# A decoder trunk in float32: all gate and up pairs by seven products, their weight sums formed on chip by accumulating transfers

## The chip, the cores and the metric

The kernel runs on one core of a Trainium2 chip. The core has TensorE (matmul, PE in the profile), VectorE (DVE), ScalarE (ACT), GpSimd (POOL) and SyncE (SP); each of them works through its own instructions in order, and semaphores join them. SBUF and PSUM are the memories on chip, HBM the one outside. The metric is the time of one execution in microseconds (us) of device time, lower is better.

## The reference

Two layers over a residual stream of 512 positions by 1024 features, in float32: one with a short convolution, one with sliding-window attention. Behind each stands the same feed-forward block, and that is what the change is about. F is 2816.

```python
def swiglu(h, w_gate_up, w_down):
    g, u = jnp.split(h @ w_gate_up, 2, axis=-1)
    return (jax.nn.silu(g) * u) @ w_down
...
ff = swiglu(rmsnorm(h, ffn_pre_norm[l]), ffn_w_gate_up[l], ffn_w_down[l])
h = h + rmsnorm(ff, ffn_post_norm[l])
```

## The kernel before

**Arithmetic.** A float32 factor is split into a high and a low part that TensorE multiplies at its fast rate. ScalarE makes the high part (a copy with rounding), VectorE the low one (the difference). A product is then three matmuls: low by high, high by high, high by low (`mm3`, L190 to L192). So every weight tile that comes from HBM (a *raw* tile, 128 x 1024) needs one instruction of ScalarE (`whi`, L454) and one of VectorE (`wlo`, L455) before it can be used.

**Gate and up.** F is cut into 22 tiles of 128 features, two tiles to a pair, 11 pairs in a layer. A pair's weights can be seen as four blocks a, b, c, d, and its product with the activations x (also four blocks) can be made with seven block products in place of eight, in the manner of Strassen and Winograd. Each of the seven needs a block of x or a sum of its blocks (a *factor*), and a block of the weights or a sum of them. Factors 1, 2 and 3 are blocks of x. Factors 4 to 7 are sums: `keep` copies the blocks out of PSUM into `part` tiles (L351, L354) and `factors` makes the sums and splits them (L366 to L375). One product of a pair is a *job* of 24 matmuls of 256 columns. Products 1, 6, 7 and 4 add up in one accumulator (X), 5 and 3 in another (Z), 2 in a third (Y); between them `take` reads the accumulator's partial sums (L872 to L883), and the next product on it has to wait for that.

Before, `PLAIN = 4`: the first four feature tiles of a layer (two pairs) are plain products. `project_first` makes tiles 0 and 1 in halves of 256 columns, so that it can start while the last quarter of the positions is still being normed; `gate_plain` makes tiles 2 and 3 at 512 columns. The factors are made while tile 2 is multiplied. The other nine pairs are made by seven products (`gate_jobs`).

**Weight sums.** Four of a pair's seven weight factors are sums of blocks. `Sums` makes them in HBM by GpSimd's transfers, a copy and then accumulating transfers (L521), long before they are fetched; `BEGIN` says at which place in the program each pair's sums start. For six pairs in a layer (`ADDED`) only two of the four sums are made in HBM, and the others by an addition on VectorE onto a raw tile (L445).

**Order.** `in_line` works through the jobs in a list: with a job's products it issues the split of the job three places on (`LINE_LEAD = 3`), and fetches a raw tile as soon as one of the `N_RAW` buffers is free. The down products of a finished round of pairs stand behind the next pair. Around the layer's start the order is written out by hand (`manual_schedule`): `second_half` and `last_tile` finish the norm tile by tile (GpSimd's power operation, VectorE's update, ScalarE's scaled copy `xn`), `turn` transposes on TensorE into a PSUM bank, and `split` (L336, L337) reads that bank for the high and the low part of x.

Of the kernel before, what the change touches and what calls it, by code (L numbers as in the profile page):

```python
# [16 lines left out]
P = 128  # L17
# [7 lines left out]
PLAIN = 4  # L25

ADDED = (0, 1, 2, 6, 7, 8)

BEGIN = {
# [4 lines left out]
}  # L34

ADDED = (0, 1, 2, 6, 7, 8)

BEGIN = {
# [4 lines left out]
}  # L43
WARM = 8
LEAD = 2
LINE_LEAD = 3

EARLY_IN, REST_IN = 2, 0
# [8 lines left out]
N_SLOT, N_WIDE, N_RAW, N_W = 43, 14, 7, 4  # L57
# [17 lines left out]
def yoco_kernel(  # L75
# [10 lines left out]
    w_gu: bass.AP,  # L86
# [143 lines left out]
    class Update:  # L230
# [3 lines left out]
        def __init__(self, mix, gain, gpres, add):  # L234
            self.mix, self.gpres, self.add = mix, gpres, add
            self.gain = gain
# [93 lines left out]
        def split(self, n, f, hf):  # L330
            if self.x[n][f] is None:
                self.x[n][f] = (slot("xhi", F32R), slot("xlo", F32R))
            hi, lo = self.x[n][f]
            c = slice(hf * 256, (hf + 1) * 256)
            src = self.banks[f % 4, hf][:, (f // 4) * 256 : (f // 4 + 1) * 256]
            nc.scalar.activation(hi[:, c], src, AF.Copy, scale=g(self.gpres[n], f))  # L336
            nc.vector.scalar_tensor_tensor(  # L337
                out=lo[:, c], in0=src, scalar=g(self.gpres[n], f), in1=hi[:, c].bitcast(F32),
# [3 lines left out]
        def keep(self, b, hf, vector=False):  # L342

            for i in range(2):
                if (i, hf, b // 2) not in self.parts:
                    self.parts[i, hf, b // 2] = slot("part")
                out = self.parts[i, hf, b // 2][:, (b % 2) * 256 : (b % 2 + 1) * 256]
                src = self.banks[b, hf][:, i * 256 : (i + 1) * 256]
                gain = g(self.gpres[0], b + 4 * i)
                if vector:  # L350
                    nc.vector.tensor_scalar(out=out, in0=src, scalar1=gain, scalar2=None,  # L351
                                            op0=ALU.mult)
                else:
                    nc.scalar.activation(out, src, AF.Copy, scale=gain)  # L354

        def factors(self):


            x = self.x[0]
            made = {p: [] for p in range(1, 8)}  # L360
            for p, k0, c in ((1, 0, 0), (2, 4, 0), (3, 4, 256)):
                made[p] = [[a[:, c : c + 256] for a in x[k0 + k]] for k in range(4)]
            for j in range(2):
                q11, q21, q12, q22 = (self.parts[i, hf, j] for hf in range(2) for i in range(2))

                nc.vector.tensor_tensor(out=q11, in0=q11, in1=q12, op=ALU.subtract)  # L366
                nc.vector.tensor_tensor(out=q12, in0=q22, in1=q12, op=ALU.subtract)
                nc.vector.scalar_tensor_tensor(out=q22, in0=q22, scalar=-1.0, in1=q11,
                                               op0=ALU.mult, op1=ALU.subtract)
                nc.vector.scalar_tensor_tensor(out=q21, in0=q22, scalar=-1.0, in1=q21,  # L370
                                               op0=ALU.mult, op1=ALU.subtract)
                for p, q in ((6, q22), (5, q11), (7, q12), (4, q21)):
                    hi, lo = halves("xt", F32R)
                    nc.scalar.activation(hi, q, AF.Copy)
                    nc.vector.tensor_tensor(out=lo, in0=q, in1=hi.bitcast(F32),  # L375
                                            op=ALU.subtract)
                    made[p] += [[a[:, c : c + 256] for a in (hi, lo)] for c in (0, 256)]
# [36 lines left out]
    class Raw:  # L414


        def __init__(self, *srcs):
            self.srcs = srcs
            self.widths = [s.shape[0] * S if len(s.shape) == 3 else D for s in srcs]
            self.n = sum(self.widths)  # L420

# [9 lines left out]

    class Job:
# [6 lines left out]
        def __init__(self, raws, run, then=None, make=None):  # L439
            self.raws, self.run, self.then, self.make = raws, run, then, make  # L440

        def add(self):
            if self.make:
                raw = self.raws[0].tile
                nc.vector.tensor_tensor(out=raw, in0=raw, in1=self.raws[1].tile, op=ALU.add)  # L445

# [1080 lines left out]
```

## Time and profile before

| what | value |
|---|---|
| time, median of three runs | 1041.82 us |
| lowest of the three | 1040.96 us |
| span of the profiled execution | 1043.2 us, 17017 instructions |
| granted TensorE clock, mean | 0.997 |
| busy: TensorE, VectorE, ScalarE, GpSimd | 99%, 73%, 53%, 16% |
| moved by DMA | 221.48 MB, 212 GB/s in the mean |
| HBM read and written | 214.08 MB, 85.98 MB |

The profiled execution is one more execution than the three timed ones; its own time is known as its span, 1.4 us over their median, and durations of single instructions come from it. Columns of a row by line are: line of the kernel, engine, operation, what is written and read, shapes and count, then busy time and mean ns of one, then the idle time of that engine just before and what ended it. In the timeline a row is start, length, engine and instruction, with the idle time before it in brackets. A row with x8 joins eight instructions of one kind.

### The profile page before, as it was taken

The numbers are of one execution on the slowest core, as the hardware profiler recorded it, in microseconds if no ns is written. First come the engines' busy times: TensorE is split into PE (matmuls) and PEld (weight loads), VectorE is DVE, ScalarE is ACT, GpSimd is POOL, SyncE is SP. The second block draws the span as 40 slices with busy tenths as digits, with TensorE's granted clock in tenths as the row PEclk, the third lists the DMA queues.
The fourth block names the chain that finished last, engine by engine and source line by source line (L and its number), as shares of the span: only waits on it lengthen the run. The fifth ranks groups of instructions, "written<-read, shape, count | busy, mean of one in ns | idle before, by whom it ended". The sixth has DMA issues, their size and how long they took to land.

```text
span 1043.2 us, 17017 instructions
## 1 busy us (share of the span) xinstructions
PE 1031.6 (99%) x6556; PEld 931.4 (89%) x6556; DVE 761.4 (73%) x1280; ACT 552.5 (53%) x994; POOL 170.6 (16%) x227
## 2 busy tenths in 40 slices
PE   9999999999999999999999999999999999999997
PEld 7888888989879899999898888889998999989986
DVE  5675645488676978776658998685886777896754
ACT  7222235746645455464466777666565554645531
POOL 0322231122201000000021554211211110000001
PEclk9999999999999999999999999999999999999999
DMA  9657798568969955337413588967789697534521
GB/s 333 229 176 242 183 321 303 135 184 266 316 232 311 348 175 195 123 120 233 172 42 98 145 250 234 311 215 223 177 283 339 197 322 246 184 125 159 173 89 80
DMA packets 61297, 221.48 MB, mean 212 GB/s; under 512 B 7200, under 2 KB 8096, under 8 KB 51488
## 3 DMA queue, kind: packets, MB, share of 16 engines
q1 hardware_dynamic: 48608, 140.04, 37.2%
q0 software_dynamic: 12032, 79.70, 29.7%
q8 instruction: 51, 0.84, 0.3%
q10 hardware_dynamic: 576, 0.66, 0.2%
q14 instruction: 30, 0.25, 0.1%
HBM read 214.08 MB, written 85.98 MB: 288 GB/s over the span
## 4 chain that ended last, share of the span: by engine, by line
PE 89%; DVE 4%; DMA 3%; issue 1%; ACT 1%; POOLq 0%; POOL 0%; DVEq 0%; SPq 0%; ACTq 0%
PE gx L192 6%; PE gx L191 6%; PE gx L190 6%; PE pmix L191 5%; PE pmix L192 5%; PE pmix L190 5%; PE gz L192 3%; PE gz L191 3%; PE gz L190 3%; PE pgu L190 3%; PE pgu L191 3%; PE pgu L192 3%; PE px L190 2%; PE px L191 2%; PE px L192 2%; PE pcub L594 2%
## 5 line engine op out<-in xcount | busy, mean ns | idle before, releaser
L455 DVE TENSOR_TENSOR wlo<-raw,whi 128x1024 fp32r<-128x1024 f32 (+1 forms) x188 | 227.7, 1214 | 94.4 <-ACT whi L454 94.4
L454 ACT ACTIVATE whi<-raw 128x1024 fp32r<-128x1024 f32 (+1 forms) x188 | 194.6, 1049 | 82.7 <-DVE raw L445 26.6
L190 PE MATMUL gx<-xt,whi 128*128 128x256 f32 x432 | 122.3, 283 | 0.0
L191 PE MATMUL gx<-xt,whi 128*128 128x256 f32 x432 | 122.3, 283 | 0.0
L192 PE MATMUL gx<-xt,wlo 128*128 128x256 f32 x432 | 122.3, 283 | 0.0
L190 PEld LDWEIGHTS gx<-xt,whi 128*128 128x128 f32 x432 | 82.9, 192 | 0.0
L191 PEld LDWEIGHTS gx<-xt,whi 128*128 128x128 f32 x432 | 82.9, 192 | 0.0
L192 PEld LDWEIGHTS gx<-xt,wlo 128*128 128x128 f32 x432 | 82.9, 192 | 0.0
L521 POOL DMA_DIRECT2D hsum<-in_w_gb_dram x84 | 55.9, 717 | 120.5 <-ACT whi L454 81.0
L872 ACT ACTIVATE st<-gx 128x256 f32<-128x256 f32 x72 | 27.5, 381 | 84.2 <-PE gx L192 84.2
L289 POOL TENSOR_TENSOR ur<-uv,mhalf 128x1 f32<-128x1 f32 x15 | 11.6, 774 | 358.3 <-DVE uv L285 358.3
L185 ACT ACTIVATE whi<-raw 128x1024 fp32r<-128x1024 f32 x30 | 31.8, 1058 | 65.3 <-PE pb L191 26.3
L190 PE MATMUL pgu<-xlo,whi 128*128 128x256 f32 (+1 forms) x192 | 61.6, 321 | 0.0
L191 PE MATMUL pgu<-xhi,whi 128*128 128x256 f32 (+1 forms) x192 | 61.1, 318 | 0.0
L192 PE MATMUL pgu<-xhi,wlo 128*128 128x256 f32 (+1 forms) x192 | 61.1, 318 | 0.0
L186 DVE TENSOR_TENSOR wlo<-raw,whi 128x1024 fp32r<-128x1024 f32 x30 | 49.7, 1665 | 2.9 <-ACT whi L185 2.9
L190 PE MATMUL pmix<-wlo,ahi 128*128 128x512 f32 (+1 forms) x136 | 51.3, 377 | 0.0
L191 PE MATMUL pmix<-whi,ahi 128*128 128x512 f32 (+1 forms) x136 | 51.2, 377 | 0.0
L192 PE MATMUL pmix<-whi,alo 128*128 128x512 f32 (+1 forms) x136 | 51.2, 377 | 0.0
L521 POOL DMA_DIRECT2D hsum<-hsum x24 | 19.2, 825 | 153.2 <-ACT whi L454 87.8
L180 DVE TENSOR_TENSOR wlo<-raw,whi 128x512 fp32r<-128x512 f32 x50 | 33.8, 722 | 12.9 <-ACT whi L179 9.6
L190 PE MATMUL gz<-xlo,whi 128*128 128x256 f32 x144 | 40.8, 283 | 0.0
(279 smaller groups left out, 3201.5 us busy)
## 6 DMA issues: line engine op xcount, KB each, us to landing
hsum<-in_w_gb_dram POOLq DMA_DIRECT2D x84, 512.0 KB, 8.8
raw<-hsum SPq DMA_DIRECT2D x72, 512.0 KB, 8.0
raw<-in_w_gb_dram SPq DMA_DIRECT2D x54, 512.0 KB, 5.5
raw<-in_w_dn_dram SPq DMA_DIRECT2D x34, 512.0 KB, 4.8
hsum<-in_w_dn_dram POOLq DMA_DIRECT2D x24, 512.0 KB, 8.0
raw<-in_w_in_dram SPq DMA_DIRECT2D x21, 512.0 KB, 7.0
hsum<-hsum POOLq DMA_DIRECT2D x20, 512.0 KB, 7.4
hsum<-in_w_dn_dram POOLq DMA_DIRECT2D x12, 768.0 KB, 10.8
```

The lines of the kernel that those rows point to most:

```text
L180: nc.vector.tensor_tensor(out=lo[:, c], in0=raw[:, c], in1=hi[:, c].bitcast(F32), op=ALU.subtract)
L185: nc.scalar.activation(hi, raw, AF.Copy)
L186: nc.vector.tensor_tensor(out=lo, in0=raw, in1=hi.bitcast(F32), op=ALU.subtract)
L190: nc.tensor.matmul(out, whi, xlo, start=start, stop=False, **kw)
L191: nc.tensor.matmul(out, whi, xhi, start=False, stop=False, **kw)
L192: nc.tensor.matmul(out, wlo, xhi, start=False, stop=stop, **kw)
L289: nc.gpsimd.tensor_tensor(out=self.r[:, t : t + 1], in0=self.v[:, t : t + 1], in1=mhalf[:, :1], op=ALU.pow)
L454: self.begun = nc.scalar.activation(hi[:, :n], raw, AF.Copy)
L455: nc.vector.tensor_tensor(out=lo[:, :n], in0=raw, in1=hi[:, :n].bitcast(F32), op=ALU.subtract)
L521: nc.gpsimd.dma_start(dst, src, max_dma_last_dim=4 * 4 * S, **kw))
L594: nc.tensor.matmul(ps, (whi, whi, wlo)[i][:, kk], (xhi, xlo, xhi)[i], start=k == i == 0, stop=k == KT - 1 and i == 2)
L872: nc.scalar.activation(s, x, AF.Copy)
```

## The change

All 11 pairs go by seven products; the plain path and its weight array are gone. Pairs 0, 1, 2 and 3 are called A, B, C and D in the new tables, so that A5 is product 5 of pair 0. A class `Gates` holds a pair. The sums are formed on chip: a raw tile is fetched with block b, an accumulating transfer from GpSimd's queue adds block a to it (product 5), a second one c (product 6), a third d (product 3); another raw tile holds c (product 1) and then c + a (product 7). Each split reads the tile between two adds, and an add has to wait until both parts of the split before it have read the tile. For the *early* pairs A and B the sum of product 3 comes from HBM, the only gate sum still made there.

The splits go in an order of their own (`READY` for the opening, `SPLIT` for later pairs), the products in another (`OPENING`, then `PAIR`). `Line` holds up to five split weights ahead (`N_W`). The factors 5, 6, 7 and 4 are made one at a time between the products of the opening. The takes now cover both halves of a pair's accumulator at once.

```diff
-PLAIN = 4
-ADDED = (0, 1, 2, 6, 7, 8)
+PAIR = (1, 5, 6, 2, 7, 3, 4)
+SPLIT = {5: -2, 1: 0, 6: 2, 2: 3, 7: 4, 3: 6, 4: 8}
+OPENING = "A3 B3 C1 C2 A5 A6 B5 A7 B6 A4 C5 B7 C6 B4 C7 C3 C4"
...
-N_SLOT, N_WIDE, N_RAW, N_W = 43, 14, 7, 4
+N_SLOT, N_WIDE, N_RAW, N_W = 40, 14, 7, 5
...
+        def add_parts(self, j):
+            q11, q21, q12, q22 = (self.parts[i, hf, j] for hf in range(2) for i in range(2))
+            nc.vector.tensor_tensor(out=q11, in0=q11, in1=q12, op=ALU.subtract)
+            nc.vector.tensor_tensor(out=q12, in0=q22, in1=q12, op=ALU.subtract)
+            nc.vector.scalar_tensor_tensor(out=q22, in0=q22, scalar=-1.0, in1=q11,
+                                           op0=ALU.mult, op1=ALU.subtract)
+
+        def factor(self, p):
+            made = []
             for j in range(2):
...
+                if p == 4:
+                    nc.vector.scalar_tensor_tensor(out=q21, in0=q22, scalar=-1.0, in1=q21,
+                                                   op0=ALU.mult, op1=ALU.subtract)
+                q = {6: q22, 5: q11, 7: q12, 4: q21}[p]
+                hi, lo = halves("xt", F32R)
+                nc.scalar.activation(hi, q, AF.Copy)
+                nc.vector.tensor_tensor(out=lo, in0=q, in1=hi.bitcast(F32), op=ALU.subtract)
...
+        def add(self):
+            if self.jobs and self.jobs[0].more is not None:
+                tc.keep_in_program_order(
+                    nc.gpsimd.dma_start(self.tile, self.jobs[0].more, accum_op=ALU.add))
...
-                nc.vector.tensor_tensor(out=raw, in0=raw, in1=self.raws[1].tile, op=ALU.add)
...
+        def lo(self):
+            job = self.begun
+            job.lo()
+            self.held += not job.apart
+            job.raw.jobs.pop(0)
+            if job.raw.jobs:
+                job.raw.add()
+            else:
+                self.live -= 1
+            self.fetch()
+            return job
...
+        def fill(self):
+            while self.jobs and self.held < N_W:
+                job = self.one()
...
+        def run(self, jobs, late):
+            for job in jobs:
+                self.fill()
+                if job.run:
+                    job.run(job)
+                    self.held -= not job.apart
...
+                c, d, a, b = (w_gb[l, q, n] for n in range(4))
+                t1, t3 = Raw(b), Raw(c)
+                last = Raw(sums_of[f"h{l}{q}"].sums[0]) if early else t1
+                for p, raw, more in ((1, t3, None), (2, Raw(d), None), (5, t1, a), (6, t1, c),
+                                     (7, Raw(c) if early else t3, a),
+                                     (3, last, None if early else d), (4, Raw(b), None)):
+                    self.jobs[p] = Job(raw, self.run(p), None, more)
...
+                elif p == 6 and self.early:
+                    add(g1, x, g1)
+                    through(g1)
...
-                    for f in range(KT):
-                        before.split(0, f, 1)
-                    for b in range(4):
-                        before.keep(b, 1)
...
+                    for f in range(4):
+                        before.split(0, f + 4, 1)
+                        before.keep(f, 1, 0)
+                        before.keep(f, 1, 1, True)
+                    line.one()
+
+            for p, k0 in ((1, 0), (2, 4)):
+                for ks in ((0, 1), (2,), (3,)) if p == 1 else ((0,), (1,), (2,), (3,)):
+                    for gate in (a, b):
+                        gate.products(p, gate.jobs[p].w, ks)
...
+            early(a, ps_pt, lambda: None)
+            early(b, ps_sc, lambda: make(5))
+            gates[2].jobs[1].then = lambda: (make(6), a.take(2), b.take(2))[3:]
+            gates[2].jobs[2].then = lambda: make(7)
+            a.jobs[5].then = lambda: (make(4), sum_on(f"{l}f3"))[2:]
```

Three places in the order of the built programs follow, without times. The first is ScalarE in the kernel before, where the last quarter of the positions (`xt` banks 1682 to 1703) has been transposed, at layer 0's start:

```order
L336 ACTIVATE xhi_1568<-xt_1703,gt 128x256
L336 ACTIVATE xhi_1583<-xt_1682,gt 128x256
L336 ACTIVATE xhi_1591<-xt_1685,gt 128x256
L336 ACTIVATE xhi_1595<-xt_1700,gt 128x256
L336 ACTIVATE xhi_1601<-xt_1703,gt 128x256
L354 ACTIVATE part_1742<-xt_1682,gt 128x256
L354 ACTIVATE part_1744<-xt_1682,gt 128x256
L354 ACTIVATE part_1742<-xt_1685,gt 128x256
```

The same place on ScalarE after (`whi_1575` and `whi_1576` are halves of B3's weights, `whi_1634` is A5's, the banks are 1651 to 1672):

```order
L308 ACTIVATE xn_1573<-h_317,ur_1140 128x1024
L460 ACTIVATE whi_1575<-raw_1331 128x512
L460 ACTIVATE whi_1576<-raw_1331 128x512
L466 ACTIVATE whi_1634<-raw_1325 128x1024
L334 ACTIVATE x_1695<-xt_1651,gt 128x256
L351 ACTIVATE part_1698<-xt_1651,gt 128x256
L334 ACTIVATE x_1702<-xt_1654,gt 128x256
L351 ACTIVATE part_1698<-xt_1654,gt 128x256
L334 ACTIVATE x_1707<-xt_1669,gt 128x256
L351 ACTIVATE part_1710<-xt_1669,gt 128x256
```

Before, all splits of the last banks stand ahead of all copies to `part`; after, split and copy take turns on each bank, four splits in place of eight, and three halves or tiles of weights stand ahead of them.

The second place is VectorE after, where the factors of layer 0 are used up: takes of product 2 for A, B and C (`gr` from `gy`), factor 7 (`xt_1901`, `xt_1904`), the split of C5, the take of A5 (from `gz`), factor 4 and the split of B6, and at the end the take of A6 (`gr_1787` from `gx_1531`), which A7 waits for:

```order
L473 TENSOR_TENSOR wlo_1867<-raw_1382,whi_1866 128x1024
L915 TENSOR_TENSOR gr_1898<-gy_1873,st_1853 128x2x256
L378 TENSOR_TENSOR xt_1901<-part_1698,xt_1901 128x512
L378 TENSOR_TENSOR xt_1904<-part_1710,xt_1904 128x512
L473 TENSOR_TENSOR wlo_1909<-raw_1465,whi_1908 128x1024
L915 TENSOR_TENSOR gr_1787<-gz_1914,gr_1787 128x2x256
L373 SCALAR_TENSOR_TENSOR part_1563<-part_1700,part_1563 128x512
L378 TENSOR_TENSOR xt_1942<-part_1563,xt_1942 128x512
L373 SCALAR_TENSOR_TENSOR part_1566<-part_1712,part_1566 128x512
L378 TENSOR_TENSOR xt_1946<-part_1566,xt_1946 128x512
L473 TENSOR_TENSOR wlo_1950<-raw_1364,whi_1949 128x1024
L915 TENSOR_TENSOR gr_1787<-gx_1531,gr_1787 128x2x256
```

The same work on VectorE before, with all four factors in one piece behind the first of the plain 512-column products:

```order
L366 TENSOR_TENSOR part_1605<-part_1605,part_1742 128x512
L367 TENSOR_TENSOR part_1742<-part_1744,part_1742 128x512
L368 SCALAR_TENSOR_TENSOR part_1744<-part_1744,part_1605 128x512
L370 SCALAR_TENSOR_TENSOR part_1607<-part_1744,part_1607 128x512
L375 TENSOR_TENSOR xt_1948<-part_1744,xt_1948 128x512
L375 TENSOR_TENSOR xt_1951<-part_1605,xt_1951 128x512
```

Before, no take of a product lies among the factors; after, the takes, the splits of other jobs and the factors follow one another on the same queue.

The third place is GpSimd after, at the same part of layer 0 (`raw_1325` becomes A5's and then A6's tile, `raw_1364` B5's and B6's):

```order
L303 TENSOR_TENSOR ur_1140<-uv_1139,mhalf 128x1
L439 DMA raw_1465<-in_w_gb_dram 128x1024
L439 DMA raw_1325<-in_w_gb_dram 128x1024
L439 DMA raw_1583<-in_w_gb_dram 128x1024
L439 DMA raw_1371<-in_w_gb_dram 128x1024
L439 DMA raw_1364<-in_w_gb_dram 128x1024
L572 DMA hsum_138<-in_w_dn_dram 64x2048
```

Before, the same queue held there:

```order
L311 TENSOR_TENSOR ur_1188<-uv_1187,mhalf 128x1
L521 DMA hsum_140<-hsum_138 64x2048
L521 DMA hsum_160<-in_w_dn_dram 64x2048
L521 DMA hsum_161<-in_w_dn_dram 64x2048
L521 DMA hsum_141<-hsum_140 64x2048
```

There the adds into raw tiles stand where the gate sums in HBM were made, and the sums for the down weights are queued among them.

More of the change, by code (lines that the diff above doesn't have):

```diff
@@ L340, in split @@
             )
[L342 to L354, printed above, removed]
@@ L694, in tile_done @@
         res.mean(t)
+        if more:
+            more()
         if t > 0:
@@ L904, in gate @@
[L904 to L933 removed]
+                    self.products(p, job.w)
@@ L1014, in ffn @@
         mix = [None] * NB
-        pss = [bank("pgu", ps_mm) for _ in range(4)]
+        factors = {p: None for p in range(1, 8)}
+        rounds = [rd for rd, (f0, f1) in enumerate(ROUNDS) for _ in range(f0, f1, 2)]
+        last = len(ROUNDS) - 1
+        gates = [Gates(q, q < 2).ending(pair_acts if rd == last else pair_sums, acts[rd])
+                 for q, rd in enumerate(rounds)]
+        opening = [gates["ABC".index(n[0])].jobs[int(n[1])] for n in OPENING.split()]
+        jobs, behind_one = [], []
@@ new lines, in ffn @@
+            for p, k0 in ((1, 0), (2, 4)):
+                for ks in ((0, 1), (2,), (3,)) if p == 1 else ((0,), (1,), (2,), (3,)):
+                    for gate in (a, b):
+                        gate.products(p, gate.jobs[p].w, ks)
+                    for k in ks:
+                        then(k0 + k)
+            line.held -= 2
+            factors[3] = before.blocks(3)
+            line.one()
+            for gate in (a, b):
+                gate.take(1)
+            before.add_parts(0)
+            before.add_parts(1)
@@ new lines, in ffn, with make, early, run @@
+            sum_on(f"{l}f1")
+            gates[2].open("X", ps_pt)
+            def make(p):
+                factors[p] = before.factor(p)
+            def early(gate, pool, after):
+                def run(job):
+                    gate.products(3, job.w, pool=pool)
+                    after()
+                    gate.take(3)
+                gate.jobs[3].run = run
+            early(a, ps_pt, lambda: None)
+            early(b, ps_sc, lambda: make(5))
+            gates[2].jobs[1].then = lambda: (make(6), a.take(2), b.take(2))[3:]
```

474 lines of the change are left out of this document (245 added, 229 removed), and 8 rows, old and new, of the table BEGIN.

## The prediction

> **What bounds the kernel now.** I read the page's shares first, then TensorE's waits, the chain, and the stretch that the change rewrites.
>
> ```profile
> span 1043.2 us, 17017 instructions
> PE 1031.6 (99%) x6556; PEld 931.4 (89%) x6556; DVE 761.4 (73%) x1280; ACT 552.5 (53%) x994; POOL 170.6 (16%) x227
> ```
>
> ```profile
> PE px L190 <- DVE mix L1002: 2.3, 1, 2.3
> PE idle L572 <- DVE mhalf L142: 1.1, 1, 1.1
> PE pcub L594 <- ACT whi L585: 0.6, 1, 0.6
> PE psc L1186 <- DVE nm L1198: 0.3, 1, 0.3
> ```
>
> TensorE is busy for 99% of the span and its waits for other engines sum to 4.3 us. So the kernel is bound by the number of matmul columns it streams, almost from end to end. Two things follow. Work taken off VectorE, ScalarE or the DMAs is worth nothing unless TensorE waits for it, and today it does not. And any wait the change puts before a TensorE instruction is paid in full, since TensorE has no slack to give it back.
>
> The price of a matmul is the distance between starts, not the busy time, because matmuls overlap. The timeline of TensorE at the place where plain products give way to the seven products shows both widths:
>
> ```profile
> 184.35 0.28 PE L190 MATMUL pgu<-xlo,whi 128*128 128x256 f32 x1
> 184.59 0.28 PE L192 MATMUL pgu<-xhi,wlo 128*128 128x256 f32 x1
> ...
> 230.22 0.39 PE L190 MATMUL pgu<-xlo,whi 128*128 128x512 f32 x1
> 230.90 0.28 PE L190 MATMUL gx<-xlo,whi 128*128 128x256 f32 x1
> ```
>
> From 184.35 to 184.59 are two steps of 256 columns, 0.120 us each; from 230.22 to 230.90 three steps of 512 columns, 0.227 each. One product of a pair (a job) is 24 matmuls of 256, 2.88 us.
>
> **The change, part by part.** *Products.* Before, the first two pairs of a layer take 192 matmuls of 256 and 96 of 512: 23.04 + 21.76 = 44.80 us. After, they take 336 of 256: 40.32. That is 4.48 us less per layer, 8.96 in both, 0.86% of the span. It is all that can be won: nothing else on TensorE shrinks. With no new wait the span is 1034.2.
>
> *Sums by accumulating transfers.* What goes and what comes, from the groups by line and the page's DMA issues:
>
> ```profile
> L445 DVE TENSOR_TENSOR raw<-raw,raw 128x1024 f32<-128x1024 f32 x24 | 29.2, 1218 | 0.0
> L455 DVE TENSOR_TENSOR wlo<-raw,whi 128x1024 fp32r<-128x1024 f32 x186 | 226.3, 1219 | 94.4 <-ACT whi L454 94.4
> L454 ACT ACTIVATE whi<-raw 128x1024 fp32r<-128x1024 f32 x186 | 193.5, 1053 | 81.4 <-DVE raw L445 26.6 <-DVE mix L1002 18.0 <-DMA raw<-hsum 10.4
> ...
> hsum<-in_w_gb_dram POOLq DMA_DIRECT2D x84, 512.0 KB, 8.8
> hsum<-hsum POOLq DMA_DIRECT2D x20, 512.0 KB, 7.4
> hsum<-in_w_dn_dram POOLq DMA_DIRECT2D x12, 768.0 KB, 10.8
> ```
>
> The 24 additions on VectorE go (29.2 us), as do most gate sums in HBM. Six more weight splits per layer come (14 for the early pairs in place of 8): 12 x 1.22 = 14.6 us of VectorE and 12.6 of ScalarE. None of this lies on TensorE's path by itself. No transfer of before accumulates into SBUF; its nearest rows are the accumulates HBM to HBM (7.4 us to landing) and the mixed group of copies and accumulates (8.8), with 10.8 for half as many bytes again. I take 8, between the first two. In the order of after, a sum's add is issued behind the low half of the split that reads the raw tile before it, and the next split of that tile stands at least three jobs, mostly four, later: 8.64 or 11.52 us. Off these go that split itself (1.05 + 1.22 and a handover of about 0.1), which leaves 6.2 or 9.1 us until ScalarE reaches the next split. ScalarE may be about 3 us late there before TensorE notices, because the next product on the same accumulator needs ScalarE's or VectorE's take only one job (2.88 us) further on. So adds of 8 us cost nothing; the ends of the range are nought, and what the last rival says. While an add waits on GpSimd's queue, the adds and down sums behind it wait too. At the layer's start the power operations of the norm stand behind three adds; the fetches of these three begin some 15 us before those operations run, so I cost that at nothing, too.
>
> *The opening.* This is where I see the loss. Before, the 21.8 us of plain 512-wide products hid the making of the factors (sums and differences of the activation blocks, and their splits). Here is what VectorE and ScalarE did in that time:
>
> ```profile
> 192.44 1.15 ACT L316 ACTIVATE xn<-h,ur 128x1024 f32<-128x1024 f32 x1
> 195.71 3.02 ACT L336 ACTIVATE xhi<-xt,gt 128x256 fp32r<-128x256 f32 x8 [2.12 <-PE xt L327]
> 198.58 3.08 ACT L354 ACTIVATE part<-xt,gt 128x256 f32<-128x256 f32 x8
> ...
> 196.22 3.23 DVE L337 SCALAR_TENSOR_TENSOR xlo<-xt,gt,xhi 128x256 fp32r<-128x256 f32 x8 [4.44 <-ACT xhi L336]
> 208.86 1.41 DVE L814 TENSOR_TENSOR gr<-pgu,gr 128x512 f32<-128x512 f32 x2 [4.16 <-ACT gr L813]
> 210.54 2.36 DVE L455 TENSOR_TENSOR wlo<-raw,whi 128x1024 fp32r<-128x1024 f32 x2 [0.26 <-ACT whi L454]
> 213.15 0.68 DVE L366 TENSOR_TENSOR part<-part,part 128x512 f32<-128x512 f32 x1
> 213.87 0.69 DVE L367 TENSOR_TENSOR part<-part,part 128x512 f32<-128x512 f32 x1
> 216.04 2.50 DVE L375 TENSOR_TENSOR xt<-part,xt 128x512 fp32r<-128x512 f32 x4
> ```
>
> Beside them two groups of ScalarE are needed below, the Silu of a pair and the high halves of the factors:
>
> ```profile
> L907 ACT ACTIVATE gr<-gr 128x512 f32<-128x512 f32 x36 | 21.7, 628 | 27.7 <-DVE gr L880 27.7
> L374 ACT ACTIVATE xt<-part 128x512 fp32r<-128x512 f32 x16 | 8.8, 620 | 13.5 <-issue 7.2 <-DVE part L368 6.2
> ```
>
> The factors were made from 213 us on and nobody waited. After, the sevenfold products start at once, and need the same factors about 20 us earlier. I follow layer 0 on before's clock, with products beginning at 184.35.
>
> First, A3. TensorE finishes products 1 and 2 of A and B (96 matmuls, 11.5 us, and the transposes, for which 230.90 - 184.35 - 44.80 leaves 1.75) near 197.6. ScalarE's idle 2.12 us is now filled by the splits of B3 and A5, whose low half holds VectorE to about 197.1. Then each of the four blocks of tile 3 goes ScalarE high, VectorE low, ScalarE keep, VectorE keep, on one PSUM bank, in turn. By the rows this is 0.38 + 0.40 + 0.39 with VectorE's keep beside the next high part, about 1.2 us a block without handovers, 1.45 with 0.1 each. The last low half ends at 200.9 to 201.9, and A3, which needs it in its fourth step, ends five steps of 0.36 us later, at 202.7 to 203.7, instead of 200.5. **Stall 2.2 to 3.2 us.**
>
> [...]
>
> Second, A5, after B3, C1 and C2 (8.64 us): TensorE is ready at 212.1 by the later clock. VectorE has, from 203.2, two splits (2.36), six differences at 0.72 (4.3), two splits (2.36) and the first low half of factor 5 (0.62): 212.9. **Stall 0.5 to 0.9.**
>
> Third, A7. It adds onto the accumulator of A6, so VectorE must have taken A6 first, and that take stands far behind on VectorE: three more low halves of factors, two takes of product 2, the split of A7, a take for C, two low halves of factor 7, the split of C5, the take of A5, all of factor 4 and the split of B6. TensorE is ready after A5, A6 and B5, at 221.6. VectorE's busy time alone from 203.2 is 22.7 us: four splits on to seven at 1.22 (8.5 in all), six differences (4.3), eight low halves (5.0), two negations (1.4), five takes of 0.69 (3.5); the last take ends at 225.9, a stall of 4.3. But the row is not free to run without gaps: A7's high part stands on ScalarE behind two Silus that wait for the takes of product 2 (0.63 each), factor 7's high part behind C's Silu, and factor 4 goes twice round VectorE, ScalarE, VectorE (0.69 + 0.62 + 0.68). Laid out in order, the takes of product 2 end at 216.1, A7's split at 219.1, C's take at 219.8, factor 7 at 222.4, the split of C5 at 224.0, the take of A5 at 224.7, factor 4 at 228.9, B6 at 230.5, the take of A6 at 231.2. **Stall 8.5 without handovers, 9.7 with them.**
>
> After that every product finds its factor and its split ready in the order, with VectorE idle again. The sum per layer: 2.2 + 0.5 + 8.5 = 11.2 at the least of this reading, 3.2 + 0.9 + 9.7 = 13.8 at the most; less 4.48 this is 6.7 to 9.3. Layer 1 has the same dependences and the same rows in its opening, so the span becomes 1043.2 + 13.4 to 18.6, 1056.6 to 1061.8. The profiled span lies 1.4 over the median of the runs shown (1041.82), so 1055.2 to 1060.4 in time; I take 1058, the middle.
>
> **The rivals.** *The opening is covered.* For it speaks that VectorE is busy only 73% and that before's factors show no wait; against it, that these 27% lie elsewhere, and that in the opening one queue in order must do 22.7 us of work in 18.4. With no stall: 1034.2, in time **1033**.
>
> *The opening costs only VectorE's busy time.* If ScalarE runs ahead so that VectorE never waits for it, A3 costs 1.2 to 2.2 and A7 4.3: 5.5 to 6.5 per layer, less 4.48, so 1045.2 to 1047.2 in span, in time **1045**.
>
> *Late adds (the slower side).* Some twenty adds in the two layers have the three-job window. Where a transfer lands more than 6.2 + 3.3 = 9.5 us after issue, ScalarE stands before the split, all takes stand behind it, and TensorE stops at the next product on that accumulator; each further microsecond costs 20. The rows give 7.4 and 8.8 as medians, so a part of the landings lies above 9.5, and 10.8 for the larger transfer. Against it: after moves far fewer bytes through HBM for the gate sums. If the excess is 0.5 us in the mean: 10 us on top, **1068**; at 10.8 it would be 1084.
>
> [...]
>
> *Not doing what it says* would be a sum that is still made in HBM; the order shows none but for product 3 of A and B, so I give it nothing.
>
> **How the numbers follow.** The forecast of 1058 has 0.46, the covered opening 0.18, the short opening 0.16, late adds 0.20. About 2% is what a measurement of this kernel can tell from no change: 1021.0 and 1062.7. Faster than 1021 is below the floor of 1033; I leave 0.02 for what I do not see. Slower than 1062.7 are the late adds and the upper edge of the forecast, some 0.10 of it: 0.30. The rest, 0.68, is within. The range goes from 1034, just above the covered case, to 1070, past the late adds' 0.5 us: about 0.07 is left out below and 0.12 above. The forecast alone has 1055 to 1063.
>
> **What would show it.** Right: TensorE waits for VectorE's lower half or keep at A3's first matmuls (2 to 3 us per layer), and for VectorE's take of A6 (L915) before A7 (8 to 10 us per layer), with seven-product matmuls at 0.12 us all through and about 9 us less of matmul streaming. Wrong: no such waits, and a span near 1034; or waits spread over the later pairs that end with a raw tile's transfer, which is the slow rival. If A7's wait is near 4 us, ScalarE was ahead of VectorE and I priced the handovers too high.

## The result, and the profile after

The kernel with the change takes 1067.56 us (median of four runs, 1066.57 to 1069.37) against 1042.82 before. The ratio is 1.023, with a 95% interval of 1.0205 to 1.0256: slower by 2.3%. Of the four runs behind the 1042.82 one took 3606.11 us, and the other three lie between 1040.96 and 1043.83. The forecast was 1058, with a range of 1034 to 1070; the time lies in the range, 9.6 us above the forecast, and the change came out in the class "slower by over 2%", to which I had given 0.30.

The head of the profiled execution's page:

```profile
span 1065.2 us, 17100 instructions
PE 1033.8 (97%) x6652; PEld 939.3 (88%) x6652; DVE 755.6 (71%) x1192; ACT 555.6 (52%) x946; POOL 194.4 (18%) x231
```

TensorE's busy time has hardly changed, but the span has. Its waits for other engines (in all, times, longest, in us), the four longest rows:

```profile
PE gx L181 <- DVE gr L915: 12.7, 2, 6.4
PE gz L181 <- DVE x L335: 2.8, 4, 0.8
PE px L181 <- DVE mix L1031: 2.4, 4, 0.9
PE gz L181 <- DVE part L348: 2.2, 2, 1.1
```

The first row is A7 in the two layers: each time TensorE stands for 6.4 us until VectorE has taken A6. The second and the fourth are A3. The same two places in TensorE's timeline of layer 0, with the idle time before an instruction in brackets:

```profile
199.39 0.36 PE L181 MATMUL gz<-x,whi 128*128 128x256 f32 x1 [1.05 <-DVE part L348]
201.11 0.39 PE L181 MATMUL gz<-x,whi 128*128 128x256 f32 x1 [0.77 <-DVE x L335]
202.53 0.58 PE L181 MATMUL gz<-x,whi 128*128 128x256 f32 x1 [0.80 <-DVE x L335]
...
224.24 0.28 PE L183 MATMUL gz<-xt,wlo 128*128 128x256 f32 x1
230.88 0.55 PE L181 MATMUL gx<-xt,whi 128*128 128x256 f32 x1 [6.36 <-DVE gr L915]
231.66 0.41 PE L181 MATMUL gx<-xt,whi 128*128 128x256 f32 x1
```

These rows hold a second thing. From 230.88 to 231.66 are three steps of 0.26 us in the mean, and the steps behind them are 0.21 us each in place of 0.12; the length of a matmul has grown from 0.28 to 0.41. TensorE itself is slow after the wait. The busy time by stretches has the granted clock in the column before the last two (the columns are TensorE, its weight loads, VectorE, ScalarE, GpSimd, clock, share of the DMA engines and GB/s):

```profile
197.00:204.00 7.00, 4.38 (x28) 3.80 (x27) 4.37 (x10) 4.01 (x9) 1.72 (x2) 0.84 0.99 207
204.00:213.00 9.00, 9.00 (x60) 9.00 (x60) 8.86 (x11) 5.97 (x9) 2.00 (x4) 0.74 0.70 157
216.00:224.00 8.00, 8.00 (x69) 8.00 (x68) 4.96 (x8) 5.28 (x8) 1.39 (x2) 1.00 0.98 314
224.00:232.00 8.00, 1.64 (x10) 1.47 (x9) 5.09 (x8) 3.44 (x5) 2.19 (x3) 0.82 1.04 244
232.00:240.00 8.00, 8.00 (x54) 8.00 (x53) 6.17 (x7) 2.97 (x5) 1.65 (x2) 0.75 0.96 254
```

At A3's waits and at A7's the clock goes to half for some microseconds. With the stretches cut finer it is 1.00 from 198.34 to 201.79 us and 0.50 from 201.79 to 208.62: it falls when A3's third wait is 0.06 us old, so that the two waits of 1.05 and 0.77 us were enough for it. Summed over the starts of the matmuls, each start later than 0.12 us after the last, that costs 2.7 and 2.1 us in layer 0 and 2.6 and 1.9 in layer 1.

Where the 22.0 us of span came from, counted by the starts of matmuls: the gaps at A3 and A7 are 10.1 us in layer 0 and 10.0 in layer 1 (their waits of 9.0 and 8.8, and the slow first steps behind these), the matmuls at the slow clock lose 4.7 and 4.5 more; that is 29.3. The first block began 0.6 us later, 29.9; the saving of the matmuls takes 8.96 off: 20.9. The other 1.1 us I leave unassigned. The waits of the down products (`px`) are in sum as long as before, 2.4 us against 2.3. But before it was one wait, which ended at 298.15, and the clock was 0.50 from 299.6 to 302.9 us behind it; the 1.7 us lost there are not lost after. Against these stand three short waits of the later pairs after, which end at 279.54, 389.24 and 450.20 us and cost 1.5 us.

### The profile page after: what moved, and what is told of

Read it like the earlier page. It is cut to its first block, busy times and chain, and to the rows that moved or that the text cites. A ratio compares the mean times of both kernels' runs of the same rounds, so it can differ in the third digit from the quotient of the medians.

```text
span 1065.2 us, 17100 instructions
## 1 busy us (share of the span) xinstructions
PE 1033.8 (97%) x6652; PEld 939.3 (88%) x6652; DVE 755.6 (71%) x1192; ACT 555.6 (52%) x946; POOL 194.4 (18%) x231
## 4 chain that ended last, share of the span: by engine, by line
PE 82%; DVE 6%; issue 4%; ACT 4%; DMA 2%; POOL 1%; POOLq 0%; DVEq 0%; SPq 0%; ACTq 0%
PE gx L181 7%; PE gx L182 7%; PE gx L183 7%; PE pmix L182 4%; PE pmix L181 4%; PE pmix L183 4%; PE gz L181 3%; PE gz L183 3%; PE gz L182 3%; PE px L181 2%; DMA raw<-in_w_gb_dram 2%; PE px L182 2%; PE px L183 2%; PE pcub L644 2%; DVE wlo L473 2%
## 5 line engine op out<-in xcount | busy, mean ns | idle before, releaser
L473 DVE TENSOR_TENSOR wlo<-raw,whi 128x1024 fp32r<-128x1024 f32 x209 | 253.7, 1218 | 106.7 <-ACT whi L466 105.6
L466 ACT ACTIVATE whi<-raw 128x1024 fp32r<-128x1024 f32 x209 | 217.2, 1048 | 114.9 <-DMA raw<-in_w_gb_dram 52.7
L181 PE MATMUL gx<-xt,whi 128*128 128x256 f32 x528 | 152.1, 288 | 13.7 <-DVE gr L915 12.7
L439 POOL DMA_DIRECT2D raw<-in_w_gb_dram x84 | 72.9, 870 | 465.4 <-DVE wlo L473 252.6
L182 PE MATMUL gx<-xt,whi 128*128 128x256 f32 x528 | 151.4, 287 | 0.0
L181 PEld LDWEIGHTS gx<-xt,whi 128*128 128x128 f32 x528 | 103.5, 196 | 14.6 <-issue 14.3
L182 PEld LDWEIGHTS gx<-xt,whi 128*128 128x128 f32 x528 | 103.5, 196 | 0.0
L176 ACT ACTIVATE whi<-raw 128x1024 fp32r<-128x1024 f32 x31 | 32.8, 1058 | 58.6 <-PE pu L182 25.0
L181 PE MATMUL gz<-x,whi 128*128 128x256 f32 x176 | 53.1, 302 | 5.0 <-DVE x L335 2.8
L182 PE MATMUL gz<-x,whi 128*128 128x256 f32 x176 | 52.2, 297 | 0.0
L183 PE MATMUL gz<-x,wlo 128*128 128x256 f32 x176 | 52.2, 296 | 0.0
L177 DVE TENSOR_TENSOR wlo<-raw,whi 128x1024 fp32r<-128x1024 f32 x31 | 47.2, 1527 | 4.6 <-ACT whi L176 4.5
L181 PE MATMUL gy<-x,whi 128*128 128x256 f32 x176 | 50.3, 286 | 0.0
L181 PE MATMUL gz<-xt,whi 128*128 128x256 f32 x176 | 49.8, 283 | 0.0
L182 PE MATMUL gz<-xt,whi 128*128 128x256 f32 x176 | 49.8, 283 | 0.0
L183 PE MATMUL gz<-xt,wlo 128*128 128x256 f32 x176 | 49.8, 283 | 0.0
```

The lines of the kernel that those rows point to most:

```text
L176: nc.scalar.activation(hi, raw, AF.Copy)
L177: nc.vector.tensor_tensor(out=lo, in0=raw, in1=hi.bitcast(F32), op=ALU.subtract)
L181: nc.tensor.matmul(out, whi, xlo, start=start, stop=False, **kw)
L182: nc.tensor.matmul(out, whi, xhi, start=False, stop=False, **kw)
L183: nc.tensor.matmul(out, wlo, xhi, start=False, stop=stop, **kw)
L439: nc.gpsimd.dma_start(self.tile, self.jobs[0].more, accum_op=ALU.add))
```

## The experiments

Two theories stood against each other at first. One: the end of the opening is set by VectorE's queue up to the take of A6, so that only what shortens that queue helps. The other: each wait costs for itself. A third possibility was that transfers that add into raw tiles come late.

The changed kernel's trace has its first gate product at 184.95 us, those of the first four runs below have it between 182.93 and 183.11, whatever their edit. So some 2 us of what their spans are shorter lie ahead of the opening and belong to no edit; what each edit did is read from the places in the opening.

**Splits ahead of the copies.** All four splits of tile 3 first, then the copies to `part`:

```diff
 for f in range(4):
     before.split(0, f + 4, 1)
-    before.keep(f, 1, 0)
-    before.keep(f, 1, 1, True)
+for f in range(4):
+    before.keep(f, 1, 0)
+    before.keep(f, 1, 1, True)
```

> All four splits of tile 3 stand ahead of the copies to part, so that they no longer take turns on a bank. Theory (the end of the opening is set by VectorE's queue, up to the take of A6): A3's waits of 2.6 us and the slow clock after them go in each layer, but A7 then waits longer; what is won is only by how much VectorE's queue gets ahead, about 2.9 us per layer (the four blocks in 3.2 us in place of 5.8 or so). So 1067.6 - 6 = about 1062, with A7's wait near 8 us. Rival (each wait costs for itself, with its slow clock): 2.6 + 2.8 per layer less, 1067.6 - 11 = about 1057, A7's wait unchanged at 6.4.

Measured 1059.42 us, 8.1 less, between the two. But the places decide: A3's wait fell from 2.6 to 1.6, its slow clock went, and A7's wait *rose* from 6.4 to 7.1 us, though TensorE reached it earlier. Counted from the first product, A7 starts 42.5 us later against 45.9 in layer 0: 3.4 us won, and 3.2 in layer 1, near the 2.9 by which I had VectorE's queue shorter, not the 5.4 of two separate costs. That the two engines took turns on a bank was a real cost, on VectorE's queue. In the changed kernel each of VectorE's four copies waited for ScalarE's copy out of the same bank, and the four blocks took it from 197.74 to 203.49 us, 5.8 us. One of the four:

```profile
198.76 0.48 DVE L348 TENSOR_SCALAR part<-xt,gt 128x256 f32<-128x256 f32 x1 [0.54 <-ACT part L351]
```

With the splits ahead they take 3.2 us, without a gap:

```profile
195.79 1.65 DVE L335 SCALAR_TENSOR_TENSOR x<-xt,gt,x 128x256 fp32r<-128x256 f32 x4
197.36 1.65 DVE L348 TENSOR_SCALAR part<-xt,gt 128x256 f32<-128x256 f32 x4
```

**Factor 4 later.** It is made behind the take of A6:

```diff
-a.jobs[5].then = lambda: (make(4), sum_on(f"{l}f3"))[2:]
+a.jobs[5].then = lambda: sum_on(f"{l}f3")
+a.jobs[6].then = lambda: (make(4),)[1:]
```

> Factor 4 is made behind the take of A6 and not behind A5, so that the take of A6 comes 4.1 us earlier on VectorE. Theory: A7's wait falls from 6.4 to 2.2 us in each layer, A4 still finds factor 4 ready, and the time falls by 8 us to about 1059; the slow clock after the shorter wait stays. Rival: the wait moves on to A4, which needs factor 4, and the time stays within 3 us of 1067.6.

Measured 1059.25. A7's wait is 2.0 us in each layer, as the theory said, and no slow clock follows it directly. A new wait of 1.8 us before A4, for A7's own take, was not foreseen; behind it the clock is at half.

**Both.**

> Both edits. Theory: what they bring adds up, since both shorten VectorE's way to the take of A6: 2.9 + 4.1 = 7 us per layer, 1067.6 - 14 = about 1054, with A7's wait near 4 us and none at A3. Rival (waits for themselves): 11 + 8 = 19 less, about 1049.

Measured 1052.81, 14.8 less, nearer to the theory. In the profile the opening has these waits left:

```profile
PE gx L181 <- DVE gr L915: 4.8, 2, 2.8
PE gz L181 <- DVE part L348: 3.6, 2, 2.0
PE gx L181 <- DVE st L915: 2.5, 3, 1.8
```

**No adds.** The 84 transfers that add into raw tiles are left out.

```diff
 def add(self):
     if self.jobs and self.jobs[0].more is not None:
-        tc.keep_in_program_order(
-            nc.gpsimd.dma_start(self.tile, self.jobs[0].more, accum_op=ALU.add))
+        pass
```

> The accumulating transfers into raw tiles are left out, 84 in all (so the products 5, 6, 7 and 3 use single blocks in place of sums). Theory: none of them is late, ScalarE's waits for them cost TensorE nothing, and the time stays within 2 us of 1067.6. Rival (late adds): the waits in the later pairs and the opening that hang on them go, and the time falls by 10 us or more.

Measured 1064.55 (1063.54 to 1065.30), 3.0 less. A7's waits are not shorter without the adds (13.5 us in the two layers together, against 12.7). Of the 3.1 us between the two spans 2.0 lie ahead of the first gate product, and the three runs above, which have their adds, are that much shorter there, too. So the adds had at most some 3 us of the 25, by the traces about 1; the rival's 10 or more are ruled out for this order of the opening.

**A7 two jobs later**, behind C5 and B6, with both edits of the opening (the order of the splits, `READY`, is changed in the same way):

```diff
-OPENING = "A3 B3 C1 C2 A5 A6 B5 A7 B6 A4 C5 B7 C6 B4 C7 C3 C4"
+OPENING = "A3 B3 C1 C2 A5 A6 B5 C5 B6 A7 A4 B7 C6 B4 C7 C3 C4"
```

> Both edits of the run before (splits ahead of the copies, factor 4 behind the take of A6), and product A7 two jobs later, behind C5 and B6, its weight split behind theirs. Theory: the wait for the take of A6 is what is left of the opening (2.4 us per layer); with 5.8 us more of products ahead of it it goes, and the wait of 1.8 us for A7's own take before A4 stays or grows somewhat; 1052.8 - 5 to - 9, about 1046. Rival (what is left is not the order of A7 but VectorE's total work, which then shows at the next product): a wait of the same size stands at A4 or B7, and the time stays within 2 us of 1052.8.

Measured 1056.89, 4.1 *more* than without it. My theory fell. The wait that the rival named is there, though the time lies outside both. A7's wait is gone, but A4 then waits 5.3 us in each layer for A7's take, which is now as far back on VectorE:

```profile
PE gx L181 <- DVE st L915: 10.9, 3, 5.3
```

This order of the products does not help; what is left to try is a shorter queue on VectorE, or fewer gaps in it.

**Waits put into the kernel before.** To price the slow clock alone, VectorE multiplies the low half of one product's weights by one, n times, ahead of eight products of the steady part:

```diff
+WAITS = {(0, 1, 2): 1, (0, 3, 2): 2, (0, 5, 2): 3, (0, 7, 2): 4, (1, 1, 2): 5, (1, 3, 2): 6, (1, 5, 2): 8, (1, 7, 2): 10}
...
 whi, wlo = job.w
+for _ in range(WAITS.get((l, q, p), 0)):
+    nc.vector.tensor_scalar(out=wlo, in0=wlo.bitcast(F32), scalar1=1.0,
+                            scalar2=None, op0=ALU.mult)
```

> The kernel before, with a wait put in ahead of product 2 of eight pairs in its steady part: VectorE multiplies the low half of that product's weights by one, 1, 2, 3 and 4 times in layer 0 and 5, 6, 8 and 10 times in layer 1. About 1.1 us for each, so waits of some 1 to 11 us. What the clock does after them: theory (a slow clock needs a few us of idle TensorE close together): none after waits below some 3 us, and 2 to 3 us lost in matmuls at 0.21 us after each longer one, whatever its length. Rival (the slow clock comes of the dense 256-column products in the opening and not of waits): no slow matmuls anywhere. The time is 1042.8 plus the sum of the waits plus 2 for each long one, by the rival without these.

Measured 1107.75 us in one run. One multiplication added some 0.6 us, and each stood behind other work in VectorE's queue (the first began 2.9 us after TensorE had stopped), so that the eight waits were 3.65 to 9.60 us, none short. They are one row of TensorE's waits:

```profile
PE gy L193 <- DVE wlo L893: 49.5, 8, 9.6
```

The busy time and the clock in three stretches, two right behind the waits of 5.23 and 9.60 us and one some microseconds further on:

```profile
465.30:469.00 3.70, 3.70 (x17) 3.70 (x18) 0.42 (x1) 0.00 (x0) 0.00 (x0) 0.50 0.02 4
...
1016.10:1020.10 4.00, 4.00 (x21) 4.00 (x21) 0.42 (x1) 0.00 (x0) 0.00 (x0) 0.51 0.00 0
1021.00:1030.00 9.00, 9.00 (x77) 9.00 (x76) 5.80 (x7) 5.30 (x8) 0.00 (x0) 1.00 0.62 178
```

All eight waits, and nothing else but the last microseconds of the span, have a stretch at a clock of 0.50. The kernel before has the same 256-column products without the waits, and a clock of 1.00, but for one stretch of 3.4 us behind its own wait of 2.3 us. So the slow clock comes of the wait. It does not grow with it: 1107.75 - 1042.7 - 49.5 = 15.5 us for eight, 1.9 each; by the starts of the matmuls it is 16.0, between 1.5 and 2.7 for one, 1.6 behind the wait of 3.65 us and 1.6 behind that of 8.48. With the stretches cut finer, the clock falls 2.4 to 5.1 us after TensorE has stopped, from 4.84 us of wait on while TensorE still stands, and stays at half for 3.4, 6.8 or 10.2 us; so a part of a long wait's slow stretch lies in the wait itself.

Where the limit lies for short waits this run doesn't show; all fourteen traces together do in part. All 16 waits of 3.65 us and more have the slow stretch. Of nine waits of 1.78 to 2.77 us with no other wait in the 8 us ahead of them, six have it (1.5 us lost for each of the two of 2.0 us in layer 1 of the third run) and three, among them the longest, do not. Waits up to 1.65 us that stood alone have none, the first 12 us of the span left aside. Waits close together have it sooner: 1.8 us when 5.8 us of products lay between it and one of 2.0 or 2.8 us, and A3's short ones, in the changed kernel and in the second and fourth run, in both layers. Why waits of one length differ no run here shows.

The theory's limit of some 3 us was an estimate of mine, and the traces don't bear it out: the six waits of 1.78 to 2.27 us were enough, and A3's two of 1.05 and 0.77 us show that the idle time need not be in one piece.

**The gaps in VectorE's queue.** On top of both edits, the Silu of the first half of A, B and C is taken at product 7 and not at product 2, so that ScalarE's high parts of A7's weights and of factor 7 do not stand behind it; factor 4's two negations go ahead of its splits:

```diff
+for j in range(2 if p == 4 else 0):
+    q11, q21, q12, q22 = (self.parts[i, hf, j] for hf in range(2) for i in range(2))
+    nc.vector.scalar_tensor_tensor(out=q21, in0=q22, scalar=-1.0, in1=q21,
+                                   op0=ALU.mult, op1=ALU.subtract)
...
-    if p == 4:
-        nc.vector.scalar_tensor_tensor(out=q21, in0=q22, scalar=-1.0, in1=q21,
-                                       op0=ALU.mult, op1=ALU.subtract)
...
 add(g0, y, sv)
-through(g0)
+if self.q > 2:
+    through(g0)
...
 add(u, self.banks["X"], u)
+if self.q < 3:
+    through(g0)
```

> On top of the third run (splits ahead of copies, factor 4 behind the take of A6): the Silu of the first half of A, B and C is taken at their product 7 in place of product 2, so that the high parts of A7's weights and of factor 7 no longer stand behind it on ScalarE, and factor 4's two negations go ahead of its two splits. Theory (gaps in VectorE's queue, not its work alone, hold the take of A6): the gaps of 1.65 and 1.2 us there go, and 0.7 in factor 4; A7's wait (2.8 and 2.0) goes, A4's (1.8 and 0.3) mostly, and with them the slow clock: 1052.8 - 9 to - 11, about 1043. Rival (work alone): within 2 us of 1052.8.

Measured 1049.08: 3.7 less, a third of what I expected. The waits at A7 did go (0.4 us in all). In their place stand waits further on:

```profile
PE gx L181 <- DVE st L916: 6.1, 6, 1.6
```

**The first bank first.**

```diff
 for f in range(4):
     before.split(0, f + 4, 1)
+    if f == 0:
+        before.keep(0, 1, 1, True)
 for f in range(4):
     before.keep(f, 1, 0)
-    before.keep(f, 1, 1, True)
+    if f:
+        before.keep(f, 1, 1, True)
```

> The run before, and VectorE's copy out of the first bank goes directly behind that bank's split, so that the bank, which A3's accumulator uses next, is free sooner. Theory: A3's wait of 1.6 to 2.0 us shrinks by about 0.9 in each layer, the rest stays: about 2 us below the run before, near 1041, that is within 2 us of the kernel before. Rival (A3 waits for the splits, not for the bank): no change against the run before.

Measured 1049.04, the same as the run before, with a wide spread (1045.33 to 1053.33). A3's wait fell from 3.6 to 2.1 us in sum, and the profiled execution was 3.7 us shorter (1.4 of it ahead of the first gate product), but the times don't show it. What was late now had come with the run before, whose trace has it at the same place, and not the third run's. VectorE's timeline of this kernel has a long gap:

```profile
229.65 1.23 DVE L474 TENSOR_TENSOR wlo<-raw,whi 128x1024 fp32r<-128x1024 f32 x1 [3.95 <-ACT whi L467]
```

And ScalarE's has, just before it and 11 us later:

```profile
228.56 1.06 ACT L467 ACTIVATE whi<-raw 128x1024 fp32r<-128x1024 f32 x1 [5.23 <-DMA raw<-in_w_gb_dram]
239.50 1.06 ACT L467 ACTIVATE whi<-raw 128x1024 fp32r<-128x1024 f32 x1 [2.63 <-DMA raw<-in_w_gb_dram]
```

ScalarE waits for raw tiles, and VectorE for ScalarE. The transfer that ends the first of these waits is an add: it was issued at 217.62 us and landed at 228.45, 10.8 us later, over the 9.5 us that the prediction's slow rival had as its limit. That is the third possibility, late adds, which the fourth run had shown to be worth little while the opening was slow. So it was asked again.

**No adds, in the quicker opening.** The 84 adds are left out of the last kernel.

> The run before (all edits of the opening) without the accumulating transfers, so that the products 5, 6, 7 and 3 use single blocks. With TensorE's long waits gone, an add that lands late has less room. Theory (adds were covered by the opening's waits and are now late by a few us at one or two places, as VectorE's gap of 3.95 us behind ScalarE's split of a raw tile at 229.65 shows): the waits for L916 in the opening fall by 3 to 5 us in all and the time goes from 1049 to about 1044, with less spread. Rival (adds still cost nothing): within 2 us of 1049.

Measured 1041.80 (1040.84 to 1042.72), 7.2 less and with little spread. ScalarE's waits for raw tiles of gate and up, 64 us in the run before, are gone from its row, and so are TensorE's 4.8 us for L916, of which 0.8 are left. Leaving the adds out takes traffic away, too: plain fetches of gate and up weights landed in 3.7 us in the median, against 5.4. But all of the 64 us were waits for adds, none for a fetch. The adds do cost: 7 us here, at most 3 in the slow opening that hid them. The span of this run is 1039.1; the floor of 1034.2 and 3.9 us of waits left in the opening make 1038.1, so that, to within 1 or 2 us, the saving on TensorE's stream is there.

**Two attempts to win these 7 us.** Two of six differences of the activation blocks went to GpSimd:

```diff
-nc.vector.tensor_tensor(out=q11, in0=q11, in1=q12, op=ALU.subtract)
-nc.vector.tensor_tensor(out=q12, in0=q22, in1=q12, op=ALU.subtract)
+eng = (nc.vector, nc.gpsimd)[j]
+eng.tensor_tensor(out=q11, in0=q11, in1=q12, op=ALU.subtract)
+eng.tensor_tensor(out=q12, in0=q22, in1=q12, op=ALU.subtract)
```

> The run before last (all edits of the opening, adds in place), with two of the six differences of the activation blocks moved from VectorE to GpSimd, where 512 columns take 1.3 to 1.7 us against 0.69. Theory (VectorE's queue is the bound of what is left): 1.4 us less on it, 0.5 to 1.4 us per layer less wait, 1 to 3 us below 1049. Rival (GpSimd's queue is in order and already holds adds that wait): the add behind the two differences goes out later, and the time rises by 1 to 4 us.

Measured 1051.36, 2.3 more, as the rival had it, though the two intervals to the kernel before overlap (1.0063 to 1.0111 against 1.0039 to 1.0086). The trace shows a reason that neither had: VectorE's own two differences, which now run beside GpSimd's two, take 2.00 and 1.67 us in place of 0.68 and 0.69, in both layers.

```profile
201.66 1.64 POOL L363 TENSOR_TENSOR part<-part,part 128x512 f32<-128x512 f32 x1
201.86 2.00 DVE L363 TENSOR_TENSOR part<-part,part 128x512 f32<-128x512 f32 x1
203.89 1.67 DVE L364 TENSOR_TENSOR part<-part,part 128x512 f32<-128x512 f32 x1
```

From the split ahead of the differences to their end VectorE needs 7.2 us in place of 6.4, so its queue has become 0.85 us longer per layer and not 1.4 shorter. And an eighth raw buffer:

```diff
-N_SLOT, N_WIDE, N_RAW, N_W = 40, 14, 7, 5
+N_SLOT, N_WIDE, N_RAW, N_W = 38, 14, 8, 5
```

> All edits of the opening, adds in place, with an eighth raw buffer (two of the 40 512-column slots given up for its room), so that a raw tile is fetched, and its add issued, one split earlier. Theory (the 7 us that the adds cost here come of the chain buffer free, fetch landed, add issued, add landed, split): some of them go, 1049 - 2 to - 5, about 1045.5, at the kernel before or 3 us over it. Rival (the add waits for the split before it and not for the fetch): within 1.5 us of 1049.

Measured 1054.05, 5.0 more. But it brought waits in the attention part, which had lost two slots, and so its cause was not clear from itself:

```profile
PE xt L319 <- ACT xn L308: 2.1, 1, 2.1
PE po L181 <- DVE plo L1355: 1.7, 2, 1.2
```

> The run before had two edits in one: an eighth raw buffer and two slots of 512 columns fewer. This one has the two slots fewer alone, with seven raw buffers and all edits of the opening. Theory (the new waits in the attention part, 5 us in sum, come of the missing slots, and the eighth raw buffer moved nothing in the opening): about 1054, as with the eighth buffer. Rival (the eighth buffer itself did the harm): about 1049, as with 40 slots.

Measured 1052.00 (1049.85 to 1053.64), between the two. The missing slots seem to have some 3 us of it, with the wait for `plo` of 1.7 in this run, too; the eighth buffer wins nothing, and whether it costs 2 us these spreads can't say. No version with adds beat the kernel before: the best, at 1049, is 0.6% slower than it.

## Why the prediction was right, and where it was wrong

**The products.** 8.96 us less on TensorE's stream: right, as the run without adds and with the mended opening shows.

**A3.** Stall 2.2 to 3.2 us: measured 2.6 and 2.4. Turns on one bank were the cause of its second and third wait (0.77 and 0.80 us in layer 0), which are gone in the first experiment. A block took 1.42 us in the changed kernel (VectorE's L335 starts at 197.74, 199.16, 200.58 and 202.00); the 1.45 that I took had handovers of 0.1 in it, an estimate of mine. No run shows the 1.2 us that the short opening had as its least at A3: with the turns A3 waited 2.6 and 2.4 us, with the splits ahead of the copies 1.6 in layer 0. In one point the reading was wrong: the first 1.05 us of it is not for a split but for the copy out of the bank that A3's accumulator takes over (`part`, L348). With the splits ahead this wait grew to 1.6 us; with the first bank's copy first it is 0.8.

**A5.** Stall 0.5 to 0.9: none measured. VectorE was ready at 213.3 on the profile's clock, but TensorE came to A5 only at 215.7, late from its slow clock at A3.

**A7.** Stall 8.5 to 9.7: measured 6.36 in both layers, below the 8 to 10 us that were named as a sign of being right. The queue itself was laid out right. The take of A6, predicted to end at 231.2, stands here in VectorE's timeline of the changed kernel (with its first product 0.6 us later than I had put it):

```profile
224.59 0.68 DVE L373 SCALAR_TENSOR_TENSOR part<-part,part 128x512 f32<-128x512 f32 x1
225.97 0.69 DVE L378 TENSOR_TENSOR xt<-part,xt 128x512 fp32r<-128x512 f32 x1 [0.70 <-ACT xt L377]
...
228.91 1.23 DVE L473 TENSOR_TENSOR wlo<-raw,whi 128x1024 fp32r<-128x1024 f32 x1 [0.25 <-ACT whi L466]
230.05 0.68 DVE L915 TENSOR_TENSOR gr<-gx,gr 128x512 f32<-128x512 f32 x1
```

It ends at 230.7. What was late was TensorE: it came to A7 at 224.5 and not at 221.6, because it had run at half clock after A3. So this term was 2 to 3 us too large, and the sum of the next point makes up for it.

**The step that failed** is that a wait "is paid in full", by which I meant by its own length. Each of the four places of waiting cost 1.9 to 2.7 us of half clock besides, 9.2 us in all, which stands in no term of the sum. A3's part of it was mostly hidden again in A7's shorter wait, so that the two errors of sizes went against each other. That the time still lay in the range is in part luck: without it the forecast would have been further off.

**The adds.** "Adds of 8 us cost nothing": nearly right for this kernel (at most 3.0 us, by the traces about 1), landing at 6.9 us in the median and 11.1 at most, six of the 84 after more than the 9.5 us of the slow rival:

```profile
raw<-in_w_gb_dram POOLq DMA_DIRECT2D x84, 512.0 KB, 6.9
```

But it held only because the opening was slow. With the opening mended they cost 7.2. The late adds that I had as the slow rival were thus real, but second in line.

**The sum.** Stalls of 11.2 to 13.8 us per layer were forecast; gaps and slow matmuls together came to 14.8 and 14.5, two thirds gaps and one third half clock. Of the 3.4 us of span above the upper end of the forecast, 1.7 are this, and the rest is the later start and what I left unassigned. The chance of 0.30 for slower by over 2% was too low for a forecast whose upper edge, 1060.4, lay 2.3 us below the bound while all terms that could be missing were on one side.

## What to carry to other kernels

When TensorE is busy all the time, work that it does in a long plain product also hides other engines' work; before it is replaced by fewer products, lay out the queues of the other engines row by row with their gaps, and ask of each take where it stands in the queue, not only how long it takes. Price a wait of TensorE at its length, and from 3.65 us on at 1.5 to 2.7 us more, as it was here for the eight put in and for A7's two of 6.36; a wait of about 2 us, or short ones close together, may cost as much, too: here it was 1.5 us behind each of two waits of 2.0, and 2.7 and 2.6 behind A3's. When a run shows that something costs nothing, ask again after the larger wait in front of it has been taken away.

## What had not been expected

TensorE's clock was at 0.50 for 3 to 6 us after each of the waits of 3.65 to 9.60 us, and that cost about 2 us (1.5 to 2.7) whatever the length; two waits of 1.05 and 0.77 us, 0.95 us apart, did the same. Two differences given to GpSimd made VectorE's own two, beside them, two to three times as long. Transfers that add into SBUF took 6.9 us to landing for 512 KB from GpSimd's queue, less than the sums in HBM before (8.8). And the 84 adds, which cost at most 3 us in one order of the opening, cost 7 in another that differs only in the opening.
